# Staging a down pass eight steps ahead, and splitting the mixers' last contraction into an early and a late term

## The chip, the cores and the metric

The kernel runs on one core of a Trainium2 chip. The metric is the device time of one execution in microseconds (us); the figure for a kernel is the median of its runs. The core has five engines that each work through their own queue in order: TensorE (PE, matrix products; its weight loads are listed as PEld), VectorE (DVE), ScalarE (ACT), GpSimd (POOL) and SyncE (SP, which here only issues transfers). Transfers are issued from the queues of SP, ACT and POOL, and run on the core's 16 DMA engines.

## The reference

A decoder trunk of two residual layers over x of 1 x 1024 x 1024 float32. Layer A (even) is a causal differential attention beside a pooling mixer; layer C (odd) is a sliding-window attention with 16 query heads, a learned sink per head and an output projection. Each ends with a gated MLP that has a causal convolution of width 3:

```python
def swa_layer(x, norm_g, w_in, q_g, k_g, sinks, w_out):
    ...
    o = sliding_window_attention(q, k, v, sinks).astype(x.dtype)
    return x + o @ w_out

def conv_glu_ffn(x, norm_g, w_up, conv_w, conv_b, w_down):
    S = x.shape[1]
    h = rms_norm(x, norm_g) @ w_up
    hp = jnp.pad(h, ((0, 0), (CONV_W - 1, 0), (0, 0)))
    c = conv_b
    for j in range(CONV_W):
        c = c + conv_w[j] * hp[:, j:j + S]
    gate, up = jnp.split(c, 2, axis=-1)
    return x + (jax.nn.silu(gate) * up) @ w_down
```

with D_MODEL 1024 and D_FF 2816. So w_up is 1024 x 5632 and w_down 2816 x 1024.

## The kernel before

**Products.** Every float32 operand is split into a high part (an ACT copy, L130) and a low part (a DVE subtraction, L131, some on POOL), and a product is three matmuls: high by high, high by low, low by high. The MLP's products go by the seven products of Strassen's scheme on quarters, so sums and differences of quarters are formed before they are split.

**Stages**, by the time of the profiled execution: layer A 0 to 417, its up pass to 864 and down pass to about 1100; layer C to 1453, its up pass to about 1880 and down pass to the end.

**Order.** Instructions are written by the program in one order, and a scheduler moves them, engine by engine, by a simulated time and by the priorities that the code gives (`urgent(offset)`: the larger, the earlier). A tile comes from a ring of fixed size by its tag (x 8 tiles, xg 16, r 3, wr 2, ws 8, b 11, and PSUM banks s 3, q 3, d 2): who asks for a tile waits until the one that had it is done.

**The down pass** (`ffn_down`) forms the products p in the order 1, 5, 6, 3, 7, 2, 4, each over K = 11 steps k; a step is 12 matmuls of 128x512. `fetch` (L538, L545) puts the weights of a step into a staging tile by an SP transfer, from tags that `stages` lists: for product 1 the first two pairs of steps in wr, the later ones in r. The gated input comes from DRAM (gd) on POOL's queue into the tiles b, xg and hf (L551 to L570), and so does the residual x (L566). `prepare` forms the sum or difference that a product needs (`combine`, L573) and splits both operands (L130, L131). `lead`, after each step, fetches 9 steps ahead (FETCH) and prepares 3 ahead (AHEAD). The products' results are added to x on DVE (L632). In product 5 the weights' sums go into tiles that are kept (`held`, `sums`), since products 6 and 3 use them again.

**The mixers' ends.** `contract` (matmuls at L122, addition into x at L271) multiplies the attention's output by a part of the output projection, block by block (d of 8, half h of 2 of the positions), and adds each block to x. A generator yields beside the attention's main work (`weave`), so its matmuls fill the time in which TensorE would wait. In layer C the 16 heads are four groups of operands; groups 0 and 1, and then group 2 alone, are contracted beside the attention of the last group; the last group's contraction is `last`, one half at a time, with the norm of the next stage (`after`: L294 to L308) fed block by block.

Of the kernel before, what the change touches and what calls it, by code (L numbers as in the profile page):

```python
# [20 lines left out]
P = 128  # L21
# [36 lines left out]
AHEAD = 3  # L58
FETCH = 9

# [7 lines left out]
class Trunk:  # L68
# [190 lines left out]
    def contract(self, ws, gs, x, after=None, banks="dq", halves=(0, 1)):  # L259
# [4 lines left out]
        for n, (d, h) in enumerate(order):  # L264
# [7 lines left out]
                if after is not None:  # L272
                    after(d, h, xs)
                    if d == ND - 1:
                        after(None, h, None)

    def scaled_begin(self, idx, spill):
# [236 lines left out]
    def ffn_down(self, layer, xs, gd, after, begin=lambda part: None):  # L514
# [7 lines left out]
        pairs = {1: (0, lo), 6: (0, lo), 3: (K, lo), 2: (K, lo), 4: (K, hi)}  # L522
        raws, ops = {}, {}
        stages = {p: ("r", "wr", "r", "wr", "r") for p in (5, 6, 3, 7, 2)}
        stages[1], stages[4] = ("wr", "wr", "r", "r", "r"), ("r",)
        taken = dict.fromkeys(stages, 0)
# [30 lines left out]
        sums = [held[k // 2][:, (k % 2) * HALF:(k % 2 + 1) * HALF] for k in range(K)]  # L557
        x = [self.big("x") for _ in range(ND)]
        for k in range(EARLY, K):
            nc.gpsimd.dma_start(b11[k], g(k, hi))  # L560
        for k in range(K):
            if k < EARLY:
                nc.gpsimd.dma_start(b11[k], g(k, hi))
            nc.gpsimd.dma_start(b12[k], g(k, lo))  # L564
        for d in range(ND):
            nc.gpsimd.dma_start(x[d][:], xs[d * P:(d + 1) * P, :])  # L566
        for k in range(K):
            nc.gpsimd.dma_start(b22[k], g(K + k, lo))
        for k in range(K):
            nc.gpsimd.dma_start(b21[k], g(K + k, hi))  # L570

        def combine(out, a, b, op=ALU.subtract):
# [7 lines left out]

        def prepare(p, k):
            r = raws.pop((p, k))
            with self.urgent(9000):
# [8 lines left out]
                elif p == 3:  # L592
                    l, m = combine(sums[k], r, sums[k]), b22[k]
                elif p == 7:
                    l = combine(r[0], r[0], r[1])
                    m = combine(b22[k], b22[k], b12[k])
                elif p == 2:
                    l, m = r, b21[k]
                else:
                    l, m = r, combine(b21[k], b21[k], b11[k])  # L600
                ops[p, k] = operand(l), operand(m)

# [10 lines left out]
        def product(p):  # L613
# [15 lines left out]
            for m in range(4):  # L629
                xm = x[d0 + m][:, cols]  # L630
                with self.urgent(12000):
                    nc.vector.tensor_tensor(out=xm, in0=banks[p][m][:], in1=xm, op=ALU.add)  # L632
# [5 lines left out]
        def lead(n):  # L638
            if n + FETCH < len(seq):
                fetch(*seq[n + FETCH])  # L640
            if n + AHEAD < len(seq):
                prepare(*seq[n + AHEAD])

        for n in range(FETCH):
            fetch(*seq[n])
        for n in range(AHEAD):
            prepare(*seq[n])
# [343 lines left out]
    def layer_a(self, w, norm, bd, after):  # L991
# [80 lines left out]
        def last(h, after):  # L1072
            if h == 0:
                ws.extend(self.load_split(I["a_out"][2 + i]) for i in range(2))
            return self.contract(ws, [self.halves(am[i]) for i in (2, 3)], x, after, "qs" if h else "q", (h,))

# [95 lines left out]
    def layer_c(self, w0, norm, rest, xd, after):  # L1172
# [22 lines left out]

        x, sp = [], []

        def project_out():
# [3 lines left out]
            for gs in ((0, 1), (2,)):  # L1202
                ws = [self.load_split(I["c_out"][2 * g + t]) for g in gs for t in range(2)]
                yield from self.contract(ws, [m for g in gs for m in sp[g]], x, banks="d")

# [190 lines left out]
```

## Time and profile before

| what | value |
|---|---|
| runs | 2132.19, 2134.98, 2140.15 us; median 2134.98 |
| the profiled execution's own time | 2133.47 us |
| its span, first to last instruction | 2131.5 us |
| mean granted clock of TensorE | 0.982 |
| busy: PE / PEld / DVE / ACT / POOL | 2017.4 / 1718.2 / 1611.6 / 1107.7 / 257.9 us |
| moved by DMA | 216.97 MB, mean 102 GB/s |

A row of single instructions gives start and duration in us, engine, line, operation, the tile written and the tiles read, shapes and how many, and in brackets how long the engine was idle before it and what ended that. A row of a stretch gives its bounds and length, the busy time of each engine with the number of instructions, the clock granted to TensorE, the busy share of the 16 DMA engines and GB/s. A row of waits gives engine, tile and line, what it waited for, the sum, how many times, and the longest. A line's number can be that of a helper, such as L130, L131 or L271, that many places call.

### The profile page before, as it was taken

What the parts mean: (1) busy time and instruction counts of PE and PEld (TensorE: products, weight loads), DVE (VectorE), ACT (ScalarE), POOL (GpSimd) and SP (SyncE); (2) the same over time, 40 slices, a digit from 0 to 9 for tenths busy, and PEclk for the clock granted to TensorE, in tenths of its full rate; (3) what the DMA queues carried; (4) which work ended last, traced back from release to release, by engine and by line L of the source; (5) the groups of instructions that cost most, each with busy time, mean ns of one, the idle gap of its engine ahead of it and who ended that gap; (6) DMA issues with size and microseconds to landing.
All of it is one profiled execution on the core that took longest, in us unless ns stands there. A gap on an engine that the chain in (4) does not pass through costs nothing.

```text
span 2131.5 us, 28465 instructions
## 1 busy us (share of the span) xinstructions
PE 2017.4 (95%) x10440; PEld 1718.2 (81%) x10440; DVE 1611.6 (76%) x2890; ACT 1107.7 (52%) x2115; POOL 257.9 (12%) x449
## 2 busy tenths in 40 slices
PE   8999999889999999789999989898999999979999
PEld 6999877677888888678789987776788888867787
DVE  6677787877778777698863887787877777759875
ACT  5476755454445554335445876644645555444343
POOL 0322442000000002300013330200000000021000
PEclk9999999999999999999999999999999999999999
DMA  4210221302222224762421110211222222268242
GB/s 168 90 50 22 69 95 56 119 30 89 89 83 76 80 89 163 296 219 92 146 100 41 51 39 32 89 60 60 89 77 82 79 89 89 87 222 328 89 163 85
DMA packets 82333, 216.97 MB, mean 102 GB/s; under 512 B 9360, under 2 KB 9872, under 8 KB 82192
## 3 DMA queue, kind: packets, MB, share of 16 engines
q1 hardware_dynamic: 65296, 169.00, 22.9%
q0 software_dynamic: 9984, 33.56, 4.3%
q10 hardware_dynamic: 6912, 12.59, 1.6%
q8 instruction: 82, 1.34, 0.3%
q14 instruction: 59, 0.48, 0.1%
HBM read 173.17 MB, written 41.94 MB: 101 GB/s over the span
## 4 chain that ended last, share of the span: by engine, by line
PE 83%; DVE 8%; ACT 4%; issue 2%; DMA 2%; POOL 1%; SPq 0%; ACTq 0%; DVEq 0%; POOLq 0%
PE pss L339 22%; PE psq L339 12%; PE pss L610 8%; PE psq L610 6%; PE psd L679 6%; PE psd L122 6%; PE psd L610 5%; PE psd L339 4%; PE pss L679 3%; PE psq L122 3%; PE psq L852 1%; PE pss L904 1%; PE pss L750 1%; PE pss L751 1%; DMA r<-in_dram 1%
## 5 line engine op out<-in xcount | busy, mean ns | idle before, releaser
L339 PE MATMUL pss<-xg,ws 128*128 128x512 f32 x1248 | 298.6, 392 | 16.9 <-DVE xg L131 9.2
L339 PEld LDWEIGHTS pss<-xg,ws 128*128 128x128 f32 x1248 | 235.5, 189 | 69.4 <-DVE xg L131 10.0
L610 PE MATMUL pss<-ws,ws 128*128 128x512 f32 x726 | 204.3, 398 | 34.1 <-ACT ws L130 25.3
L339 PE MATMUL pss<-T,ws 128*128 128x512 f32 x912 | 224.5, 389 | 3.4 <-ACT ws L130 3.4
L339 PEld LDWEIGHTS pss<-T,ws 128*128 128x128 f32 x912 | 171.1, 188 | 39.6 <-ACT ws L130 4.3
L610 PEld LDWEIGHTS pss<-ws,ws 128*128 128x128 f32 x726 | 138.4, 192 | 66.1 <-ACT ws L130 26.9
L679 PE MATMUL psd<-ws,xg 128*128 128x256 f32 x1344 | 184.0, 285 | 2.2 <-DVE hms L688 1.7
L610 PE MATMUL psq<-ws,ws 128*128 128x512 f32 x660 | 185.3, 392 | 0.0
L679 PEld LDWEIGHTS psd<-ws,xg 128*128 128x128 f32 x1344 | 171.4, 191 | 4.7 <-DVE hms L688 2.3
L339 PE MATMUL psq<-xg,ws 128*128 128x512 f32 x696 | 169.5, 392 | 0.0
L131 DVE TENSOR_TENSOR ws<-hf,ws 128x512 fp32r<-128x512 f32 x160 | 109.6, 689 | 73.3 <-ACT ws L130 73.1
L122 PE MATMUL psd<-xg,ws 128*128 128x512 f32 x576 | 152.4, 402 | 3.7 <-DVE x L271 2.8
L339 PEld LDWEIGHTS psq<-xg,ws 128*128 128x128 f32 x696 | 131.9, 190 | 27.6
L130 ACT ACTIVATE ws<-wr 128x512 fp32r<-128x512 f32 (+1 forms) x158 | 115.5, 735 | 72.3 <-PE pss L339 33.4
L610 PEld LDWEIGHTS psq<-ws,ws 128*128 128x128 f32 x660 | 125.3, 190 | 26.4
L610 PE MATMUL psd<-ws,ws 128*128 128x512 f32 x462 | 140.2, 397 | 0.8 <-DVE ms L241 0.8
L130 ACT ACTIVATE ws<-hf 128x512 fp32r<-128x512 f32 x160 | 99.9, 629 | 76.1 <-PE psq L339 33.3
L564 POOL DMA_DIRECT2D xg<-gd x22 | 12.1, 550 | 995.8 <-PE pss L339 994.2
L131 POOL TENSOR_TENSOR ws<-wr,ws 128x1024 fp32r<-128x1024 f32 x38 | 95.0, 2508 | 287.7 <-ACT ws L130 247.0
L347 DVE SCALAR_TENSOR_TENSOR x<-x,conv,x 128x1023 f32<-128x1023 f32 x80 | 102.6, 1282 | 30.0 <-ACT x L346 29.8
L122 PEld LDWEIGHTS psd<-xg,ws 128*128 128x128 f32 x576 | 104.8, 190 | 25.2 <-DVE x L271 5.1
L130 ACT ACTIVATE ws<-xg 128x512 fp32r<-128x512 f32 x104 | 63.0, 624 | 109.1 <-PE psd L610 74.1
(258 smaller groups left out, 4105.6 us busy)
## 6 DMA issues: line engine op xcount, KB each, us to landing
wr<-in_dram SPq DMA_DIRECT2D x102, 512.0 KB, 3.6
gd<-x SPq DMA_DIRECT2D x40, 512.0 KB, 2.6
x<-in_dram SPq DMA_DIRECT2D x38, 512.0 KB, 4.4
r<-in_dram SPq DMA_DIRECT2D x34, 512.0 KB, 3.7
r<-in_dram SPq DMA_DIRECT2D x64, 256.0 KB, 3.6
xd<-x ACTq DMA_DIRECT2D x48, 256.0 KB, 2.0
xg<-gd POOLq DMA_DIRECT2D x44, 256.0 KB, 5.4
b<-gd POOLq DMA_DIRECT2D x44, 256.0 KB, 9.0
```

What stands on the lines that cost most here:

```text
L122: self.nc.tensor.matmul(out, a, b, start=(k == 0), stop=(k == n - 1))
L130: nc.scalar.activation(hi, raw, AF.Copy)
L131: (eng or nc.vector).tensor_tensor(out=lo, in0=raw, in1=hi.bitcast(F32), op=ALU.subtract)
L339: nc.tensor.matmul(bank[:], a, b, start=start and k == 0, stop=k == n - 1, skip_group_check=open)
L347: nc.vector.scalar_tensor_tensor(out=c[:, 1:], in0=hr[:, :S - 1], scalar=cw(1), in1=c[:, 1:], op0=ALU.mult, op1=ALU.add)
L564: nc.gpsimd.dma_start(b12[k], g(k, lo))
L610: nc.tensor.matmul(banks[p][m][:], l, r, start=opens and n == 0, stop=closes and n == 2, skip_group_check=p != 2)
L679: self.nc.tensor.matmul(out, a, m[:, d % 4, :], start=(n == 0), stop=(n == 23))
L750: nc.tensor.matmul(out, q[:, qs], his[m][:, ks], start=True, stop=False)
L751: nc.tensor.matmul(out, q[rows, qs], lo[rows, ks], start=False, stop=True)
L852: nc.tensor.matmul(po[:, :256], tt[:, kb * P:(kb + 1) * P], v, start=(b == 0 and t == 0), stop=(b == j and t == 1))
L904: nc.tensor.matmul(pu[:], a, b, start=d + n == 0, stop=d == ND - 1 and n == 2)
```

## The change

In `ffn_down` the weights of product 1's later steps are staged in x tiles; `fetch` runs 14 steps ahead; `prepare` is cut in two: `gather` forms the sums and differences 8 steps ahead (LEAD), `prepare` splits them, 3 ahead as before, at a higher priority; the POOL loads are written behind the first fetches, and x is taken after those x tiles.

In layers A and C the second half of the last contraction goes through the new `contract_late`: for each block, the term whose operands are older opens the bank (six banks at the start, alternately q and s), and the newer term closes it. In layer C the third group contracts only its first half beside the attention; the second half becomes the early term, and eight additions into x disappear, since both terms accumulate in one bank.

```diff
-FETCH = 9
+LEAD = 8
+FETCH = 14
...
+    def contract_late(self, early, late, x, after, h, banks="qsqsqs"):
+        nc, n = self.nc, len(banks)
+        po = {}
+        def part(d, terms, first):
+            if first:
+                po[d] = self.bank(banks[d % n])
...
+                for a, b in ((ah, bh), (ah, bl), (al, bh)):
+                    k += 1
+                    nc.tensor.matmul(po[d][:], a, b, start=first and k == 1, stop=not first and k == total)
+        for d in range(n):
+            yield 0.65 * len(early[0])
+            part(d, early, True)
+        for d in range(ND):
+            yield 0.65 * (len(late[0]) + len(early[0]))
+            part(d, late, False)
+            xs = x[d][:, h * HALF:(h + 1) * HALF]
+            with self.urgent():
+                nc.vector.tensor_tensor(out=xs, in0=po[d][:], in1=xs, op=ALU.add)
+            after(d, h, xs)
+            if d + n < ND:
+                part(d + n, early, True)
+        after(None, h, None)
...
-        stages[1], stages[4] = ("wr", "wr", "r", "r", "r"), ("r",)
+        stages[1], stages[4] = ("wr", "wr", "x", "x", "x", "x"), ("r",)
...
-        def prepare(p, k):
+        def gather(p, k):
             r = raws.pop((p, k))
             with self.urgent(9000):
...
+            parts[p, k] = l, m
+
+        def prepare(p, k):
+            l, m = parts.pop((p, k))
+            with self.urgent(12000):
                 ops[p, k] = operand(l), operand(m)
...
-                with self.urgent(12000):
+                with self.urgent(15000):
                     nc.vector.tensor_tensor(out=xm, in0=banks[p][m][:], in1=xm, op=ALU.add)
...
+            if n + LEAD < len(seq):
+                gather(*seq[n + LEAD])
...
         def last(h, after):
             if h == 0:
                 ws.extend(self.load_split(I["c_out"][6 + t]) for t in range(2))
-            return self.contract(ws, g3, x, after, "qs" if h else "q", (h,))
+                return self.contract(ws, g3, x, after, "q", (h,))
+            return self.contract_late((held, sp[2]), (ws, g3), x, after, h)
```

The lines move: splits L130/L131 become L131/L132, `combine` L573 becomes L592, `fetch` L538/L545 become L571/L578, the matmuls of `contract` L122 become L123, those of `contract_late` are L294, the transposes of layer C L1148 become L1191, the up pass's matmuls L339 become L372 and those of the down pass L610 become L634.

**SP's queue at the start of the first down pass.** in_dram is w_down; wr_8381 and wr_8423 are weights of product 5 (steps 1 and 3), r_8282, r_8284 and r_8286 those of product 1 from step 4 on (two steps each), gd the store of the gated input. Before:

```order
L545 DMA wr_8381<-in_dram 128x512 x2
L360 DMA gd_72<-x_8054 128x1024
L545 DMA wr_8423<-in_dram 128x512 x2
L538 DMA r_8282<-in_dram 128x2x512
L538 DMA r_8284<-in_dram 128x2x512
L538 DMA r_8286<-in_dram 128x2x512
L318 DMA conv_14348<-in_dram 128x176
```

With the change, where wr_8396 is product 5's step 6, r_8230, r_8236 and r_8354 its steps 0, 2 and 4, and x_8222 to x_8228 product 1's steps 4 to 10:

```order
L578 DMA wr_8396<-in_dram 128x512 x2
L578 DMA r_8230<-in_dram 128x512
L571 DMA x_8222<-in_dram 128x2x512
L571 DMA x_8224<-in_dram 128x2x512
L571 DMA x_8226<-in_dram 128x2x512
L571 DMA x_8228<-in_dram 128x512
L578 DMA r_8230<-in_dram 128x512
L578 DMA r_8236<-in_dram 128x512 x2
L578 DMA r_8354<-in_dram 128x512 x2
```

The last wr load ahead of product 1's later weights stays ahead of them, half of r_8230 joins it, and all of product 1's weights now go in one row, with product 5's behind them.

**DVE a little later, in product 1.** ws are split operands, xg_8212 to xg_8214 the kept sums of product 5, b the gated input. Before:

```order
L131 TENSOR_TENSOR ws_8384<-r_8284,ws_8384 128x512
L573 TENSOR_TENSOR b_8195<-xg_8206,b_8195 128x512
L131 TENSOR_TENSOR ws_8387<-b_8196,ws_8387 128x512
L131 TENSOR_TENSOR ws_8405<-r_8284,ws_8405 128x512
L131 TENSOR_TENSOR ws_8408<-b_8197,ws_8408 128x512
L573 TENSOR_TENSOR b_8196<-xg_8207,b_8196 128x512
L573 TENSOR_TENSOR b_8197<-xg_8208,b_8197 128x512
L131 TENSOR_TENSOR ws_8426<-r_8286,ws_8426 128x512
```

With the change:

```order
L132 TENSOR_TENSOR ws_8401<-x_8224,ws_8401 128x512
L592 TENSOR_TENSOR xg_8212<-r_8230 128x512
L592 TENSOR_TENSOR xg_8213<-wr_8333 128x512
L592 TENSOR_TENSOR b_8195<-xg_8206,b_8195 128x512
L132 TENSOR_TENSOR ws_8404<-b_8196,ws_8404 128x512
L132 TENSOR_TENSOR ws_8424<-x_8224,ws_8424 128x512
L592 TENSOR_TENSOR xg_8213<-r_8236 128x512
L592 TENSOR_TENSOR b_8196<-xg_8207,b_8196 128x512
L132 TENSOR_TENSOR ws_8427<-b_8197,ws_8427 128x512
L132 TENSOR_TENSOR ws_8447<-x_8226,ws_8447 128x512
L592 TENSOR_TENSOR xg_8214<-r_8354 128x512
```

Sums of product 5 (from r_8230, r_8236 and r_8354) now stand between the splits of product 1's steps 6, 7 and 8.

**TensorE in the tail of layer C, at the last transposes.** hf and g are split attention weights and values, L1148 (L1191) the transposes, psq and pss banks. Before:

```order
L122 MATMUL psq_14001<-g_13761,ws_13853 128x512
L122 MATMUL psq_14001<-g_13760,ws_13854 128x512
L1148 MATMUL psq_14097<-idn,t_14069 128x128 x4
L1148 MATMUL psq_14102<-idn,t_14069 128x128 x4
L122 MATMUL psq_14107<-hf_14108,g_10368 128x256
```

With the change (six rows for each of the two pss banks, all of one kind, and the last bank of the contraction's first half):

```order
L123 MATMUL psq_13925<-g_13696,ws_13790 128x512
L294 MATMUL pss_14150<-xg_13338,ws_13388 128x512
...
L294 MATMUL pss_14164<-xg_13338,ws_13395 128x512
L123 MATMUL psq_13937<-g_13696,ws_13783 128x512
...
L1191 MATMUL psq_14033<-idn,t_14005 128x128 x4
L1191 MATMUL psq_14038<-idn,t_14005 128x128 x4
L123 MATMUL psq_14043<-hf_14044,g_10368 128x256
```

Twelve matmuls of the early term now stand ahead of the transposes. Six more (pss_14136) stand earlier, and in the rest of the tail 18 stand before the split of the last group is used, and 12 behind it.

More of the change, by code (lines that the diff above doesn't have):

```diff
@@ L275, in contract @@
                         after(None, h, None)
+    def contract_late(self, early, late, x, after, h, banks="qsqsqs"):
[4 more added lines that the diff above has]
+                po[d] = self.bank(banks[d % n])
+            ws, gs = terms
+            total = 3 * len(ws)
+            k = 0
+            for (wh, wl), g in zip(ws, gs):
+                ah, al = wh[:, d * P:(d + 1) * P], wl[:, d * P:(d + 1) * P]
+                bh, bl = g(h)
+                for a, b in ((ah, bh), (ah, bl), (al, bh)):
[14 more added lines that the diff above has]
+        after(None, h, None)
     def scaled_begin(self, idx, spill):
@@ L522, in ffn_down @@
         pairs = {1: (0, lo), 6: (0, lo), 3: (K, lo), 2: (K, lo), 4: (K, hi)}
-        raws, ops = {}, {}
+        raws, parts, ops = {}, {}, {}
         stages = {p: ("r", "wr", "r", "wr", "r") for p in (5, 6, 3, 7, 2)}
-        stages[1], stages[4] = ("wr", "wr", "r", "r", "r"), ("r",)
+        stages[1], stages[4] = ("wr", "wr", "x", "x", "x", "x"), ("r",)
         taken = dict.fromkeys(stages, 0)
@@ L557, in ffn_down @@
         sums = [held[k // 2][:, (k % 2) * HALF:(k % 2 + 1) * HALF] for k in range(K)]
[L558 to L570, printed above, removed]
         def combine(out, a, b, op=ALU.subtract):
@@ L645, in ffn_down @@
             fetch(*seq[n])
+        for k in range(EARLY, K):
+            nc.gpsimd.dma_start(b11[k], g(k, hi))
+        for k in range(K):
+            if k < EARLY:
+                nc.gpsimd.dma_start(b11[k], g(k, hi))
+            nc.gpsimd.dma_start(b12[k], g(k, lo))
+        x = [self.big("x") for _ in range(ND)]
+        for d in range(ND):
+            nc.gpsimd.dma_start(x[d][:], xs[d * P:(d + 1) * P, :])
+        for k in range(K):
+            nc.gpsimd.dma_start(b22[k], g(K + k, lo))
+        for k in range(K):
+            nc.gpsimd.dma_start(b21[k], g(K + k, hi))
+        for n in range(LEAD):
+            gather(*seq[n])
         for n in range(AHEAD):
@@ L1074, in last @@
                 ws.extend(self.load_split(I["a_out"][2 + i]) for i in range(2))
-            return self.contract(ws, [self.halves(am[i]) for i in (2, 3)], x, after, "qs" if h else "q", (h,))
+                return self.contract(ws, [self.halves(am[i]) for i in (2, 3)], x, after, "q", (h,))
+            two = [([ws[i]], [self.halves(am[2 + i])]) for i in range(2)]
+            return self.contract_late(*two, x, after, h)
         ws = []
@@ L1194, in split_o @@
             return [(lambda h, t=t: (hs[h][0][:, t, :], hs[h][1][:, t, :])) for t in range(2)]
-        x, sp = [], []
+        x, sp, held = [], [], []
         def project_out():
@@ L1203, in project_out @@
                 ws = [self.load_split(I["c_out"][2 * g + t]) for g in gs for t in range(2)]
-                yield from self.contract(ws, [m for g in gs for m in sp[g]], x, banks="d")
+                if gs == (2,):
+                    held.extend(ws)
+                    yield from self.contract(ws, sp[2], x, lambda *a: None, "d", (0,))
+                else:
+                    yield from self.contract(ws, [m for g in gs for m in sp[g]], x, banks="d")
         side = dense()
```

## The prediction

> **What bounds the kernel now.** I read the page first (busy times, then the chain that ended last), then the list of what TensorE waits for, then busy time by stretch around each place that the edits touch, and last single instructions there. From the page:
>
> ```profile
> span 2131.5 us, 28465 instructions
> PE 2017.4 (95%) x10440; PEld 1718.2 (81%) x10440; DVE 1611.6 (76%) x2890; ACT 1107.7 (52%) x2115; POOL 257.9 (12%) x449
> PE 83%; DVE 8%; ACT 4%; issue 2%; DMA 2%; POOL 1%; SPq 0%; ACTq 0%; DVEq 0%; POOLq 0%
> ```
>
> PE is busy 2017.4 of 2131.5 us and is 83% of the chain. No edit removes a matmul, so all there is to win is PE's 114 us without work and the slow clock that follows its gaps. From the list of waits of the whole run, the two rows on the down pass:
>
> ```profile
> PE pss L610 <- ACT ws L130: 25.3, 4, 12.0
> PE pss L610 <- DVE ws L131: 8.8, 3, 4.1
> ```
>
> 34 us in two down passes. Where they lie, by stretch (length, then busy time of PE, PEld, DVE, ACT, POOL, granted clock, DMA share, GB/s); the first five rows are the first pass, the last two the second:
>
> ```profile
> 870.00:883.00 13.00, 1.44 (x5) 0.88 (x4) 7.09 (x8) 4.18 (x6) 6.35 (x12) 0.71 1.01 370
> 883.00:904.00 21.00, 21.00 (x87) 16.63 (x86) 17.55 (x30) 9.66 (x18) 7.74 (x15) 0.94 1.03 399
> 904.00:935.00 31.00, 29.73 (x132) 24.30 (x131) 29.97 (x50) 10.19 (x19) 0.83 (x2) 1.00 0.78 272
> 935.00:941.00 6.00, 1.85 (x6) 1.24 (x7) 6.00 (x11) 2.96 (x6) 0.00 (x0) 0.66 0.57 186
> 941.00:1100.00 159.00, 156.45 (x700) 129.29 (x699) 125.18 (x205) 76.47 (x136) 5.45 (x4) 0.98 0.35 118
> ...
> 1905.00:1920.00 15.00, 2.96 (x12) 2.11 (x11) 7.97 (x8) 4.99 (x7) 7.56 (x15) 0.66 0.98 350
> ...
> 1942.00:1975.00 33.00, 29.42 (x129) 23.71 (x127) 31.18 (x52) 12.24 (x22) 1.50 (x3) 0.99 0.73 259
> ```
>
> Each pass has two holes. The first (870 to 883) has all 16 DMA engines full: TensorE waits for weights. The second (935 to 941) has DVE at 6.00 of 6: TensorE waits for sums and splits. DVE is full for the 31 us before it too. After 941 PE is at 156.45 of 159: nothing is left there.
>
> **The down pass: the first hole.** Its instructions:
>
> ```profile
> 867.51 0.69 DVE L573 TENSOR_TENSOR xg<-wr 128x512 f32<-128x512 f32 x1 [6.39 <-PE pss L339]
> ...
> 868.24 0.81 SPq L545 DMA_DIRECT2D wr<-in_dram  x2
> 869.09 3.35 SPq L538 DMA_DIRECT2D r<-in_dram  x3
> ...
> 880.06 0.63 ACT L130 ACTIVATE ws<-r 128x512 fp32r<-128x512 f32 x1 [7.48 <-DMA r<-in_dram]
> 883.79 0.63 ACT L130 ACTIVATE ws<-r 128x512 fp32r<-128x512 f32 x1 [0.59 <-DMA r<-in_dram]
> 887.54 0.63 ACT L130 ACTIVATE ws<-r 128x512 fp32r<-128x512 f32 x1 [1.56 <-DMA r<-in_dram]
> ...
> 882.21 1.22 PE L610 MATMUL pss<-ws,ws 128*128 128x512 f32 x2 [11.56 <-ACT ws L130]
> 1918.90 1.22 PE L610 MATMUL pss<-ws,ws 128*128 128x512 f32 x2 [12.04 <-ACT ws L130]
> ```
>
> The combine at 867.51 reads a wr tile; only then may SP's next wr load go (868.24), and the loads of product 1's later weights, which TensorE needs, stand behind it on the same queue (869.09). They land 3.7 us apart per 512 KB (880.06, 883.79, 887.54), about 141 GB/s, because POOL's loads of b and x run beside them; by queue for 870 to 900, POOL's is q0:
>
> ```profile
> q0 software_dynamic: 2271, 7.82, 68.1%
> q1 hardware_dynamic: 1986, 3.80, 34.1%
> ```
>
> The change gives these weights an x tile instead of an r tile, but r was not what they waited for. In the changed order the wr load that waits for the same combine still stands ahead of them, and one more 256 KB load of product 5 with it. 256 KB at 141 GB/s is 1.9 us: the first hole grows from 11.6 to 13.5 us, in both passes. POOL's loads keep their order until long after, so they leave no more bandwidth.
>
> **The down pass: between the holes.** With sums eight steps ahead, three sums of product 5 stand on DVE, an in-order queue, ahead of splits that product 1 needs: one ahead of step 6's, one ahead of step 7's, one ahead of step 8's. What they read lands behind all of product 1's weights: from 881.9 (880.04 and 1.9) there are 512, 512, 256, 256, 512 and 512 KB to the last, 2.5 MB at 141 GB/s, so 18.6 us: 900.6. Before, DVE had only this wait there:
>
> ```profile
> 895.38 0.69 DVE L573 TENSOR_TENSOR xg<-r 128x512 f32<-128x512 f32 x1 [3.46 <-DMA r<-in_dram]
> 895.99 0.68 DVE L573 TENSOR_TENSOR xg<-wr 128x512 f32<-128x512 f32 x1
> ...
> 939.49 0.69 DVE L131 TENSOR_TENSOR ws<-b,ws 128x512 fp32r<-128x512 f32 x1
> ...
> 903.67 0.69 PE pss L610 x3
> ...
> 940.24 2.08 PE pss L610 x4
> ...
> 944.87 0.91 PE pss L610 x4
> ```
>
> From 895.38 to 939.49, the split that lets product 6 begin at 940.24, DVE does 71 operations, 0.62 us each. In the changed order 64 operations lie between the sum that waits for 900.6 and the same split: 64 × 0.62 = 39.7, so 940.3. By TensorE: step 8 of product 1 waits for about 902.5, steps 8 to 10 are 36 matmuls (12 take 2.73 us, row 864.76 below), so product 5 begins near 910 where it began at 903.67, and its 11 steps of 2.73 end at 940. Both ways product 6 begins where it did.
>
> So the second hole's 5.4 us move forward into product 1 (about 5 us) and the first hole (1.9); the sum is +0.1. What goes is the slow clock after the long gap at 936: product 6's first step took 4.63 us (940.24 to 944.87) instead of 2.73, −1.9. The three new gaps are shorter, 1 to 3 us; the row 1422 below shows half clock after two gaps of 1.19 and 1.71 us, so I charge +1.3 for them. Per pass −0.5, two passes **−1**. The bounds: if no sum is late, product 5 begins at 905.6 (903.67 and 1.9) and product 6, if DVE allows, 30.0 later, 4.6 sooner than before, with the clock's 1.9: −6.5. If the weights land as computed and the second hole stays too, +7.
>
> The Trainium skill, page "TensorE: Matmul & The Clock Gate", section "What's actually happening", has the clock halved only after an idle window of about 3.4 us. This trace shows the half clock after gaps of 1.19 and 1.71 us close together. By the page the new gaps would cost no clock, and the two passes would give −3.6 instead of −1.
>
> **Layer A's contraction.** The order of TensorE's instructions there is the same before and after: six banks already stood open with their older term, since the scheduler had moved it forward. Zero, and nothing to lose.
>
> **Layer C's contraction.** Side blocks of the third output group, 48 matmuls of the second half, leave the stretch before 1417 and go into the tail. The rows (chain of waits, then TensorE's and DVE's instructions, then stretches):
>
> ```profile
> 864.76 2.73 PE pss L339 x12
> ...
> 1397.90 2.75 PE psd L122 x12
> ...
> 1404.11 2.72 PE psd L122 x12
> ```
>
> ```profile
> L271 DVE TENSOR_TENSOR x<-psd,x x8: 678/684/692, 1400.3 to 1416.7; 128x512 f32<-128x512 f32 x8
> ```
>
> ```profile
> 1398.00:1420.00 22.00, 20.67 (x105) 17.29 (x103) 18.80 (x49) 12.41 (x34) 0.00 (x0) 1.00 0.17 56
> 1422.00:1424.00 2.00, 2.00 (x9) 1.81 (x9) 1.97 (x10) 1.04 (x4) 0.00 (x0) 0.50 0.70 246
> ```
>
> ```profile
> 1418.77 0.38 PE L122 MATMUL psq<-hf,g 128*128 128x256 f32 x1 [1.19 <-ACT hf L130]
> 1421.57 1.65 PE L122 MATMUL psq<-hf,g 128*128 128x256 f32 x6 [1.71 <-DVE hf L131]
> 1432.64 0.39 PE L122 MATMUL psq<-hf,g 128*128 128x256 f32 x1 [1.61 <-ACT hf L130]
> 1437.92 0.85 PE L122 MATMUL psq<-hf,g 128*128 128x256 f32 x5 [0.34 <-DVE hf L131]
> 1440.72 0.50 PE L122 MATMUL psq<-g,ws 128*128 128x512 f32 x1 [0.98 <-ACT g L130]
> 1452.78 1.40 PE L339 MATMUL pss<-xg,ws 128*128 128x512 f32 x5 [0.89 <-DVE x L271]
> ```
>
> What leaves: to 1410 TensorE sets the pace, and 24 of the 48 matmuls are on the chain (1397.90 and 1404.11): 5.5 us. From there DVE does, and four of its eight psd additions (0.6 us each by the spacing at 895.38) go: 2.4. Together 7.9; the attention's own DVE work (18.80 of 22 us) will not let all of it through, so I take 6.5.
>
> What comes: of the 48, six go into the 1.71 us wait (free); 12 (2.7 us) stand ahead of the last transposes, whose result is awaited at 1432.64; I count half of that 1.61 us as slack, so +1.8. Six (1.4 us) enter where 0.34 us was idle: +0.9, with some slack behind them. Twelve (2.7) fill the wait for the split g, 1.95 us from the last attention product to 1440.72: +0.8. The last 12 stand behind 1440.72 beside the 48 of the late term, which fill 10.9 of the 12.1 us to 1452.78; the rest is the last block's addition, which still follows: +2.7. Sum +6.2. The slow clock at 1422 may go with its gap (half of 1.5): −0.7. C gives −6.5 + 6.2 − 0.7 = **−1**; the bounds are −9 (all leaves, the waits hide all that comes) and +6 (nothing leaves but the work).
>
> **Sum.** −1 − 1 = −2 against the profiled execution, 2133.47 us (span 2131.5 and 2 around it): 2131.5. It stands 1.5 below the median of the runs, 2134.98, so I write 2132.
>
> **Rivals.** *The holes close.* The sums for product 6 are there in time and product 1's three waits do not come, because loads land sooner than at 141 GB/s; the first hole stays as it is. Then per pass the second hole (5.4 and 1.9 of clock) goes, and C keeps −1: 2133.5 − 14.6 − 1 = 2118. For it: DVE had 3.46 us free at 895. Against: DMA at 1.03 with POOL taking two thirds to 904, and DVE full to 941.
>
> *The early sums block.* In-order DVE waits for product 5's staged weights as computed, and the second hole stays because sums for product 6 now stand ahead of its first splits. Per pass +1.9 + 5 + 0: with the tail of C at +1, 2148. It decides if the last of the three loads lands after about 900 and more than 70 DVE operations remain. For it: the landings. Against: the order shows 64 operations, and adds and splits ahead of sums.
>
> *C alone gains.* The waits of C take up nearly all that comes, −7, and the passes give −1: 2125.5. For it: 6.7 us of idle in six rows. Against: the last 12 matmuls have no idle to go into.
>
> **How the numbers follow.** No change 0.52, the holes close 0.19, the early sums block 0.17, C alone 0.12. A measurement here tells 0.5% (10.7 us) from no change: faster is below 2124.3, slower above 2145.6. Faster: 0.19 and a third of C alone, 0.23. Slower: 0.17 and 0.02 of the forecast's upper end, 0.19. Same: 0.58. The likeliest case alone spans 2124 to 2141; to leave out no more than 2 in 10 the range reaches half into both outer rivals: 2119 to 2146.
>
> **What would show it.** Right: a wait of 13 to 14 us before step 4 of product 1 in both passes; then waits of 1 to 3 us in product 1 on DVE's splits; product 6 beginning without a wait near 940 and at full clock; in C, TensorE done with the late term some 2 to 3 us later than DVE's spare additions save. Wrong: the first wait at or below 11.6 us, no wait in product 1 after its step 4, a wait of 4 us still before product 6, or the stage from 1393 to 1453 more than 4 us shorter or longer.

## The result and the profile after

The changed kernel takes 2121.6 us (median of its runs) where the kernel before, timed beside it, takes 2133.59: a ratio of 0.9939, 95% interval 0.9923 to 0.9956. So it is faster, by 12 us. Executions far above the others of their kernel (here one of five, at 2288.93 us, and later the profiled one of e16, at 6568.74) are left out. The profiled execution took 2124.41 us, the longest of those counted; before it was 2133.47. From the page of the changed kernel:

```profile
span 2122.2 us, 28436 instructions
PE 2016.3 (95%) x10440; PEld 1719.0 (81%) x10440; DVE 1602.0 (75%) x2882; ACT 1107.2 (52%) x2115; POOL 257.8 (12%) x449
```

TensorE does the same 10440 matmuls in 1.1 us less, and the span is 9.3 us shorter: most of the gain is in TensorE's gaps. The place of a gain is found fastest by the start of the first matmul of each stage. The rows of this table are differences of such starts, in us (the last row ends with the start of the last matmul):

| stretch | before | after | difference |
|---|---|---|---|
| start to layer A's up pass | 417.60 | 417.01 | −0.6 |
| layer A's up pass | 433.85 | 433.76 | −0.1 |
| its down pass, products 1, 5, 6 | 119.55 | 119.74 | +0.2 |
| its down pass, the rest | 131.00 | 130.95 | 0.0 |
| layer C, to its up pass | 350.77 | 350.48 | −0.3 |
| layer C's up pass | 434.89 | 426.69 | **−8.2** |
| its down pass, products 1, 5, 6 | 119.95 | 119.66 | −0.3 |
| its down pass, the rest | 119.45 | 119.45 | 0.0 |

No edit is in an up pass, and yet 8.2 of the 9.3 us are in one. The places that were edited (the mixers of A and C, and the two down passes) give 1.0 us together.

**The down pass.** TensorE's waits in the changed kernel (sum, times, longest):

```profile
PE pss L634 <- ACT ws L131: 27.0, 2, 13.5
PE pss L634 <- DVE ws L132: 7.3, 5, 2.9
```

The two rows add up to 34.3 us; the corresponding rows of before had 25.3 and 8.8, so 34.1. The waits were moved, not removed. Single instructions of the first pass (TensorE; then the sums of product 5 on DVE):

```profile
883.46 1.22 PE L634 MATMUL pss<-ws,ws 128*128 128x512 f32 x2 [13.49 <-ACT ws L131]
895.11 1.95 PE L634 MATMUL pss<-ws,ws 128*128 128x512 f32 x4 [2.69 <-DVE ws L132]
903.00 1.20 PE L634 MATMUL pss<-ws,ws 128*128 128x512 f32 x4 [0.54 <-DVE ws L132]
892.55 0.69 DVE L592 TENSOR_TENSOR xg<-r 128x512 f32<-128x512 f32 x1 [5.40 <-DMA r<-in_dram]
900.45 0.69 DVE L592 TENSOR_TENSOR xg<-r 128x512 f32<-128x512 f32 x1 [1.51 <-DMA r<-in_dram]
```

The first wait has grown from 11.56 to 13.49 us, and product 1 has new waits while DVE stands before sums whose weights have not landed. By stretch, in the columns of the prediction's rows:

```profile
870.00:883.00 13.00, 0.00 (x0) 0.00 (x0) 5.16 (x7) 2.93 (x4) 6.24 (x12) 0.68 1.01 372
883.00:904.00 21.00, 17.30 (x56) 13.30 (x57) 13.30 (x21) 7.73 (x14) 5.36 (x10) 0.79 1.03 396
904.00:935.00 31.00, 31.00 (x137) 25.36 (x136) 31.00 (x53) 12.06 (x21) 2.65 (x5) 1.00 0.69 251
935.00:941.00 6.00, 6.00 (x28) 4.99 (x27) 5.82 (x10) 3.03 (x6) 0.00 (x0) 1.00 0.37 131
```

The second hole is gone: TensorE is busy all of 935 to 941, at full clock. But 883 to 904, where it was busy all 21 us, has 3.7 us without work and a clock of 0.79. Product 6 begins at 940.58; before, its second hole ended at 940.24.

**Layer C's up pass.** Before, TensorE ran into the second half's norm here:

```profile
1469.00 0.60 PE L239 MATMUL psd<-idn,hf 128*128 128x128 f32 x4
1478.33 0.50 PE L339 MATMUL pss<-xg,ws 128*128 128x512 f32 x1 [2.13 <-ACT xg L130]
1484.11 1.65 PE L339 MATMUL pss<-xg,ws 128*128 128x512 f32 x3 [4.59 <-DVE xg L131]
```

The row of 1469.00 is the transposes of that norm; the two waits behind it, 2.13 and 4.59 us, are for the scaled and split x of the second half. After:

```profile
1437.97 2.50 PE L294 MATMUL psq<-g,ws 128*128 128x512 f32 x5 [2.55 <-DVE g L132]
1451.94 8.55 PE L372 MATMUL pss<-xg,ws 128*128 128x512 f32 x37
1460.33 0.60 PE L240 MATMUL psd<-idn,hf 128*128 128x128 f32 x4
1477.72 0.98 PE L372 MATMUL pss<-xg,ws 128*128 128x512 f32 x3 [1.54 <-DVE xg L132]
```

The transposes stand 37 matmuls into the up pass instead of 71 (1460.33 less 1451.94 is 8.4 us; before, 1469.00 less 1452.78 was 16.2), and one wait of 1.54 us is left of 6.72. The same 40 us from the up pass's first matmul, before and then after:

```profile
1453.00:1493.00 40.00, 33.28 (x139) 26.89 (x139) 29.51 (x57) 13.29 (x22) 0.00 (x0) 0.87 0.09 33
```

```profile
1452.00:1492.00 40.00, 38.46 (x176) 31.62 (x175) 29.36 (x57) 15.10 (x25) 0.00 (x0) 1.00 0.19 66
```

176 matmuls against 139. The 139 took 33.28 us at a clock of 0.87; at the later kernel's 38.46/176 they would take 30.4. So 2.9 us of slow clock and 5.2 us of waits are gone: 8.1 of the 8.2.

**Why the norm comes sooner.** Rows of ACT and DVE at the end of layer C, before:

```profile
1439.61 1.06 ACT L130 ACTIVATE g<-t 128x1024 fp32r<-128x1024 f32 x1
1440.69 0.60 ACT L254 ACTIVATE rbc<-psd 128x512 f32<-128x512 f32 x1
1441.84 5.38 DVE L308 SCALAR_TENSOR_TENSOR x<-x,par,rbc 128x512 f32<-128x512 f32 x8
```

and after:

```profile
1430.76 0.60 ACT L255 ACTIVATE rbc<-psd 128x512 f32<-128x512 f32 x1 [2.47 <-PE psd L251]
1432.15 1.06 ACT L131 ACTIVATE g<-t 128x1024 fp32r<-128x1024 f32 x1
1431.39 5.39 DVE L341 SCALAR_TENSOR_TENSOR x<-x,par,rbc 128x512 f32<-128x512 f32 x8 [2.24 <-ACT rbc L255]
1436.69 1.22 DVE L132 TENSOR_TENSOR g<-t,g 128x1024 fp32r<-128x1024 f32 x1
```

rbc is the first half's norm factor, spread over the partitions; g is the last attention group's second half, being split; the eight scalings apply rbc to the first half of x. Before, ACT did g first and rbc behind it, so DVE's 5.4 us of scalings fell behind the split of g and right ahead of the eight additions (L271) that the second half's norm waits for. These began from 1447.14 to 1456.74, with the splits of the scaled x between them. Now rbc comes first, ten us earlier, and the scalings stand ahead of the split of g; the additions (L304) begin from 1442.64 to 1452.70. I call these two orders *late* (before) and *early* (after). The scheduler chose the order; no line of the change asks for it.

### The profile page after: what moved, and what is told of

Same layout as the page of the kernel before. It is cut to its first block, busy times and chain, and to the rows that moved or that the text cites. A ratio compares the mean times of both kernels' runs of the same rounds, so it can differ in the third digit from the quotient of the medians.

```text
span 2122.2 us, 28436 instructions
## 1 busy us (share of the span) xinstructions
PE 2016.3 (95%) x10440; PEld 1719.0 (81%) x10440; DVE 1602.0 (75%) x2882; ACT 1107.2 (52%) x2115; POOL 257.8 (12%) x449
## 4 chain that ended last, share of the span: by engine, by line
PE 82%; DVE 7%; ACT 4%; DMA 3%; issue 2%; POOL 1%; SPq 0%; ACTq 0%; DVEq 0%; POOLq 0%
PE pss L372 22%; PE psq L372 12%; PE pss L634 7%; PE psq L634 6%; PE psd L720 6%; PE psd L123 5%; PE psd L372 5%; PE psd L634 4%; PE pss L720 3%; PE psq L123 2%; PE psq L893 1%; DMA b<-gd 1%; PE pss L945 1%; PE pss L791 1%; PE pss L792 1%
## 5 line engine op out<-in xcount | busy, mean ns | idle before, releaser
L372 PE MATMUL pss<-xg,ws 128*128 128x512 f32 x1248 | 297.0, 391 | 10.8 <-DVE xg L132 6.1
L372 PEld LDWEIGHTS pss<-xg,ws 128*128 128x128 f32 x1248 | 234.5, 189 | 62.3 <-DVE xg L132 7.0
L634 PE MATMUL pss<-ws,ws 128*128 128x512 f32 x726 | 209.5, 398 | 34.3 <-ACT ws L131 27.0
L372 PE MATMUL pss<-T,ws 128*128 128x512 f32 x912 | 224.6, 390 | 3.4 <-ACT ws L131 3.4
L372 PEld LDWEIGHTS pss<-T,ws 128*128 128x128 f32 x912 | 171.1, 188 | 39.6 <-ACT ws L131 4.2
L634 PEld LDWEIGHTS pss<-ws,ws 128*128 128x128 f32 x726 | 138.0, 192 | 66.1 <-ACT ws L131 27.9
L634 PE MATMUL psq<-ws,ws 128*128 128x512 f32 x660 | 191.5, 393 | 0.0
L372 PE MATMUL psq<-xg,ws 128*128 128x512 f32 x696 | 168.5, 391 | 0.0
L132 DVE TENSOR_TENSOR ws<-hf,ws 128x512 fp32r<-128x512 f32 x160 | 109.6, 689 | 73.4 <-ACT ws L131 73.1
L372 PEld LDWEIGHTS psq<-xg,ws 128*128 128x128 f32 x696 | 131.1, 188 | 27.2
L131 ACT ACTIVATE ws<-wr 128x512 fp32r<-128x512 f32 (+1 forms) x156 | 114.2, 737 | 68.9 <-PE pss L372 23.7
L634 PEld LDWEIGHTS psq<-ws,ws 128*128 128x128 f32 x660 | 125.4, 190 | 26.4
L634 PE MATMUL psd<-ws,ws 128*128 128x512 f32 x462 | 145.6, 397 | 0.8 <-DVE ms L242 0.8
L123 PE MATMUL psd<-xg,ws 128*128 128x512 f32 x528 | 140.2, 404 | 3.1 <-DVE x L272 2.3
L131 ACT ACTIVATE ws<-hf 128x512 fp32r<-128x512 f32 x160 | 100.0, 630 | 76.1 <-PE psq L372 33.3
L132 POOL TENSOR_TENSOR ws<-wr,ws 128x1024 fp32r<-128x1024 f32 x38 | 95.0, 2506 | 284.8 <-ACT ws L131 242.3
L123 PEld LDWEIGHTS psd<-xg,ws 128*128 128x128 f32 x528 | 97.1, 192 | 23.2 <-DVE x L272 4.3
L372 PE MATMUL psq<-T,ws 128*128 128x512 f32 x456 | 115.6, 390 | 0.0
```

The costliest lines, as they stand in the source:

```text
L123: self.nc.tensor.matmul(out, a, b, start=(k == 0), stop=(k == n - 1))
L131: nc.scalar.activation(hi, raw, AF.Copy)
L132: (eng or nc.vector).tensor_tensor(out=lo, in0=raw, in1=hi.bitcast(F32), op=ALU.subtract)
L372: nc.tensor.matmul(bank[:], a, b, start=start and k == 0, stop=k == n - 1, skip_group_check=open)
L634: nc.tensor.matmul(banks[p][m][:], l, r, start=opens and n == 0, stop=closes and n == 2, skip_group_check=p != 2)
```

## The experiments

All kernels were timed against the kernel before on the same chip. C is the stretch from layer C's start to its up pass, and *tail* the part of it from the matmul that uses the last transposes (1432.64 before) on. P0 and P1 are products 1, 5 and 6 of the two down passes. All stretches are from one profiled execution.

| kernel | median us | ratio, 95% | C | its tail | up pass C | P0 | P1 | order in C |
|---|---|---|---|---|---|---|---|---|
| before | 2133.59 | | 350.8 | 20.1 | 434.9 | 119.6 | 120.0 | late |
| after | 2121.6 | 0.9939, 0.9923–0.9956 | 350.5 | 28.2 | 426.7 | 119.7 | 119.7 | early |
| after_again | 2123.39 | 0.9944, 0.9926–0.9961 | 349.3 | 28.1 | 426.7 | 119.6 | 120.0 | early |
| e1_staging_only | 2133.25 | 0.9997, 0.9987–1.0007 | 347.9 | 20.1 | 434.5 | 119.8 | 119.8 | late |
| e2_deferral_only | 2132.42 | 0.9994, 0.9984–1.0003 | 349.7 | 23.6 | 435.6 | 121.7 | 119.8 | late |
| e5_adds_kept | 2133.89 | 0.9996, 0.9987–1.0005 | 351.3 | 21.6 | 434.5 | 121.6 | 119.5 | late |
| e4_left_out | 2127.64 | 0.9967, 0.9954–0.9979 | 346.5 | 20.1 | 433.6 | 120.1 | 119.5 | late |
| e17_order_only | 2134.29 | 0.9994, 0.9982–1.0006 | 360.4 | 26.8 | 426.0 | 119.7 | 120.1 | early |
| e16_deferral_order | 2128.71 | 0.9964, 0.9952–0.9975 | | | | | | early |
| e16b_deferral_order | 2129.63 | 0.9974, 0.9961–0.9987 | 356.2 | 31.2 | 426.0 | 119.8 | 119.9 | early |
| e22_order_in_a | 2131.58 | 0.9978, 0.9967–0.9989 | 355.5 | 26.6 | 426.6 | 120.6 | 119.2 | early |
| e24_sums_on_pool | 2123.94 | 0.9936, 0.9918–0.9954 | 356.2 | 30.1 | 426.0 | 114.8 | 113.8 | early |
| e12_sums_on_pool_r | 2121.05 | 0.9937, 0.9919–0.9955 | 346.7 | 28.1 | 426.6 | 120.5 | 122.4 | early |
| e23_sums_on_pool_c | 2114.66 | 0.9909, 0.9893–0.9925 | 350.6 | 29.9 | 428.0 | 114.6 | 115.0 | early |

(e16b is the kernel of e16 again, on another chip, for its stretches.) C ahead of its tail differs between executions even where ACT and DVE do the same in the same order: by 3.0 us between before and e17, and by up to 3.8 us among after, after_again and e12. Differences of C of that size are not read below; the tail, the up pass and the medians are.

### Each half alone

The staging without the mixers' edits, and the mixers' edits without the staging:

```diff
# e1: the changed kernel, with the mixers as before, for instance
-            return self.contract_late((held, sp[2]), (ws, g3), x, after, h)
+            return self.contract(ws, g3, x, after, "qs" if h else "q", (h,))
# e2: the kernel before, with contract_late and its calls in layers A and C
```

> The change without its mixer part: the down pass as changed, both layers' contractions as before. Theory A (the gain comes from layer C's third group alone, whose second half leaves the attention; staging gives nothing): within 2 us of the kernel before, first wait of each down pass 13.5 us, product 5 about 7 us later than before and product 6 where it was. Theory B (the staging gives part of it, above all in the second pass): 4 us or more below the kernel before.

> The kernel before with the mixer part alone: down pass as before, first wait 11.6 us, and 4 to 5 us before product 6. Theory A: 9 us below the kernel before, all of it between layer C's last contraction and the end of the second norm's first use (the up pass of layer C from 434.9 to about 427 us). Theory B: 5 us or less.

Measured: neither gains (0.9997 and 0.9994, both intervals across 1), yet together they give 0.9939. If gains were additive, the two would give −0.1%. In e1 the down pass shows the changed kernel's waits, and the up pass those of before (waits of 850 to 1100, then of 1449 to 1500):

```profile
PE pss L634 <- ACT ws L131: 13.5, 1, 13.5
...
PE pss L372 <- DVE xg L132: 4.2, 1, 4.2
PE pss L372 <- ACT xg L131: 2.1, 1, 2.1
```

In e2, ACT has the late order, though the deferred matmuls fill the tail there too:

```profile
1433.86 1.06 ACT L130 ACTIVATE g<-t 128x1024 fp32r<-128x1024 f32 x1
1435.34 0.60 ACT L254 ACTIVATE rbc<-psd 128x512 f32<-128x512 f32 x1 [0.42 <-PE psd L250]
```

Each of the two theories fails on one run: A on e2, which was to gain 9 us, and B on e1, which was to gain 4 or more. So the gain belongs to neither edit; what both together have is the early order. That leaves two questions: does the order make the gain, and what does the deferral do for it?

### Is the deferral's gain in the additions or the matmuls?

e5 keeps the deferral in layer C but adds into x twice per block, as before; e4 leaves the 48 deferred matmuls out altogether. In both, layer A is left as before.

```diff
# e5, against e2
-            return self.contract_late((held, sp[2]), (ws, g3), x, after, h)
+            def both():
+                yield from self.contract(held, sp[2], x, lambda *a: None, "s", (1,))
+                yield from self.contract(ws, g3, x, after, "qs", (1,))
+            return both()
# e4, against e2: the third group's second half isn't contracted at all
+            return self.contract(ws, g3, x, after, "qs", (h,))
```

> As the deferral alone, but the third group's second half goes through banks of its own in the tail and is added to x by eight additions on VectorE, as before. Theory A (what counts is that the matmuls leave the stretch before the first half's last block, so that the first norm and then the second come earlier): 6 to 9 us below the kernel before; the wait in the up pass of layer C stays under 3 us. Theory C (what counts is that eight additions, 4.8 us of VectorE, are gone): at most 3 us below the kernel before, and the wait back near 6.7 us.

> As the deferral alone, but the third group's second half of layer C is not computed at all (48 matmuls, 10.9 us of TensorE, are left out). If the moved matmuls lie fully in TensorE's waits: the time of the deferral alone. If they lie on the path: 11 us below it. Theory A, from the tail of the changed kernel (TensorE 12.00 of 12 us busy at the end, waits of 2.6 us left): about half, 5 us below it.

Measured: e5 is no faster than before (0.9996), with C 1.7 us longer than in e2, which is less than two executions of the same order can differ by. e4's 48 matmuls are 10.9 us of TensorE at 2.73 us per 12; leaving them out brings the tail 3.5 us and the up pass 2.0 us below e2, and the medians 4.8 us. So about half of them lie on the path, as expected. Both kernels have the late order, and in both the up pass is within 1.3 us of before, so neither the additions nor the matmuls are where the 8.2 us went.

### The order alone, with and without the deferral

A one-column copy on ACT that reads rbc and writes to the place where the split of g goes makes ACT do rbc first. It adds 0.2 us of work and changes nothing that is computed, since the split overwrites it.

```diff
+        def rest():
+            self.nc.scalar.activation(pairs[1][0][:, 0, 0:1], self.nrbc[:, 0:1], AF.Copy)
+            cut(1)
...
-        self.finish(x, main, side, last, after, RATES_C[3], lambda: cut(1))
+        self.finish(x, main, side, last, after, RATES_C[3], rest)
# e17: on the kernel before.  e16, e16b: on e2
```

> The kernel before with the forced order alone, neither edit of the change. Theory D: the up pass of layer C shorter by 7 to 8 us; the tail of layer C up to 2 us longer, since the last split comes later; 5 to 8 us below the kernel before. Theory F (the order helps only with the deferral, which puts matmuls into the wait for the split): 3 us or less.

> The deferral alone (down pass as before) with one forced order: a one-column copy on ScalarE makes the split of the last group's second half wait for the broadcast of the first half's norm. Theory D (the gain is that order: the norm's broadcast ahead of the split, so that the eight scalings and then the second half's norm come earlier; the two edits only happened to bring it about together): 8 us below the kernel before, the up pass of layer C near 427 us and its wait near 1.5 us. Theory E (the gain needs the staged down pass itself): as the deferral alone, within 3 us of the kernel before.

> The deferral with the forced order once more, for its profile (the first one's profiled execution was disturbed): wait in the up pass of layer C near 1.5 us, that up pass near 427 us, layer C's own length within 2 us of the changed kernel's; down passes as in the kernel before.

> The changed kernel once more, beside the two others: 11 to 13 us below the kernel before, and the same times of its stages within 1 us.

Measured: the order shortens the up pass by 8.9 us in both (426.0), so the up pass is explained: it hangs on the order alone. What the order costs stands in layer C. In e17 that grows by 9.6 us and nothing is won (0.9994), as the theory had it by which the order helps only with the deferral. 3.0 of the 9.6 lie ahead of the tail, where every engine has the order of before, and are chance; the tail is longer by 6.6. TensorE there (the last group's contraction):

```profile
1445.09 0.50 PE L122 MATMUL psq<-g,ws 128*128 128x512 f32 x1 [2.01 <-ACT g L130]
1450.33 2.50 PE L122 MATMUL psq<-g,ws 128*128 128x512 f32 x5 [3.16 <-DVE g L131]
```

It waits for g, which now stands behind the scalings, and has nothing else to do. With the deferral it has: the 48 matmuls do not need g. e16 and e16b gain 0.36% and 0.26% without any staging; e16's interval is clear of those of e17 and e2, e16b's overlaps them slightly. They do not reach the changed kernel, timed again beside e16b: C is 6.9 us longer than there, against 2 expected. 3.1 us of it are in the tail, because the forced order is a stricter one than the scheduler's own. From e16b, ACT and TensorE:

```profile
1434.73 0.60 ACT L254 ACTIVATE rbc<-psd 128x512 f32<-128x512 f32 x1 [1.51 <-PE psd L250]
1435.60 1.06 ACT L130 ACTIVATE g<-t 128x1024 fp32r<-128x1024 f32 x1
1441.94 2.50 PE L293 MATMUL psq<-g,ws 128*128 128x512 f32 x5 [3.57 <-DVE g L131]
```

Counted from the tail's start, rbc comes 1.9 us later than in the changed kernel, where TensorE does the broadcast that it reads (L251) ahead of five attention matmuls and six of the early term; g waits for it, and TensorE for g, 3.57 us instead of 2.55. The other 3.8 us lie ahead of the tail. There ACT and DVE of the two kernels go through the attention in different orders, from some 195 us into the layer on; whether that or chance makes the 3.8 us is not shown.

So this much is shown: the early order takes 8 to 9 us out of the up pass, and lengthens C's tail by 6.6 us where nothing is deferred. With the deferral the kernel gains by the order, by the medians. Part of that is the wait that the deferred matmuls fill: TensorE waits 2.55 us for g in the changed kernel, 2.01 and 3.16 in e17. The larger part is ahead of the tail: there e2, e16b and the changed kernel are 4.6, 5.7 and 8.3 us shorter than before, and the changed kernel's 8.3 are what its tail, 8.0 longer, costs. As e1, which defers nothing, is 2.9 us shorter there, how much of this the deferral gives is known only roughly. What is not shown at all is why the scheduler finds the early order only with the staging. It works in the program's order with simulated times, and the down passes that the staging edits lie before and after layer C; e12 below, another edit in the down pass on top of e2, tips it as well. I found no rule in it.

### The same order in layer A

Layer A's end is built alike and has the late order in all these kernels: its up pass is 434 us, C's early one 427. e22 forces it there (and, as in e16, in C), on the changed kernel.

```diff
-        mixes = [self.big("x") for _ in range(AH - 1)] + [self.big("rbc")]
+        mixes = [self.big("x") for _ in range(AH - 1)] + [self.big("xg")]
...
+        def rest():
+            self.nc.scalar.activation(am[3][0][:, HALF:HALF + 1], self.nrbc[:, 0:1], AF.Copy)
+            self.split_half(mixes[3], am[3], 1)
```

> The changed kernel with the same order forced in layer C (where it already is) and in layer A, where the last head's result moves from the tile that the norm's broadcast needs into an xg tile. Theory D: layer A's up pass loses its 2.1 and 4.6 us waits as layer C's did: 6 to 8 us below the changed kernel, about 2114. Against it: layer A's tail is longer by the later split, and less than 3 us are left.

Measured: A's up pass does shorten, 433.8 to 428.0 us, but it starts at 425.19 instead of 417.01, so the two together lose 2.4; with C's forced order, 355.5 instead of 350.5, the kernel is slower than the changed one (0.9978), where 6 to 8 us of gain on it were expected. The row that says why:

```profile
414.38 1.12 PE L926 MATMUL psd<-idn,xg 128*128 128x128 f32 x4 [11.38 <-DVE xg L918]
```

In A the scalings and the first half's splits stand ahead of DVE's own work on the last head, and TensorE waits 11.38 us for that. That nothing is left in A which could be deferred to cover it is argued, not tried.

### What bounds the first hole: sums on GpSimd

The staging in x tiles moved the down pass by 0.2 us. To see what it is worth once DVE's in-order queue is out of its way, product 5's sums of weights go to GpSimd: in e24 on e22, in e23 on the changed kernel with the order in C forced, and in e12 on e2, so with product 1's weights in r tiles as before.

```diff
-                    l = combine(sums[k], r[0], r[1], ALU.add)
+                    l = sums[k]
+                    nc.gpsimd.tensor_tensor(out=l, in0=r[0], in1=r[1], op=ALU.add)
```

> The kernel of the run with the order in layer A, with product 5's eleven sums of weights on GpSimd instead of VectorE. If product 1's waits come from sums that stand ahead of its splits on VectorE (as predicted and seen), they go, and eleven operations (6.6 us) leave the full stretch of VectorE: product 6 begins 6 to 8 us earlier in each pass, 12 us or more below that run, about 2102. If GpSimd's sums hold up the loads that stand behind them on its queue, the first wait grows from 13.5 us and the gain is below 3 us.

> The changed kernel with product 5's sums of weights on GpSimd and the order of layer C forced (as the changed kernel has it by itself); layer A as changed. From the run with the order in layer A: the first wait falls from 13.5 to about 6.5 us and product 3 begins 5 to 6 us sooner after the pass's start, in both passes. If that adds to layer C's gain: 11 us below the changed kernel, near 2110. If the scheduler gives layer C another order, or GpSimd's sums are late for product 5: 2115 or more.

> The deferral with product 5's sums on GpSimd, but product 1's weights staged in r tiles as before the change. If the x tiles bring nothing (as the run of the staging alone shows) and the loads' place on SP's queue is what counts: within 2 us of the run with the x tiles, first wait 6.5 us or less. If with the sums out of VectorE's way the deeper staging comes to bear: 4 us or more above it.

Measured: in e24 and e23, P0 and P1 shorten by 4.7 to 5.9 us each (against e22 and the changed kernel), and e23 is the fastest kernel of the study: 2114.66 us, 0.9909, some 9 us below the changed kernel on the same chip. Both gain less than expected (e24 7.6 us on e22 instead of 12 or more, e23 9 instead of 11); the last section shows what may be part of the reason. e23's wait for product 1's weights in the first down pass:

```profile
PE pss L635 <- ACT ws L131: 6.4, 1, 6.4
```

The first wait is 6.4 us where it was 13.49. The reason stands on SP's queue; the changed kernel first, with the sum on DVE that its wr load waits for:

```profile
859.28 0.33 SPq L393 DMA_DIRECT2D gd<-x  x1
867.55 0.80 SPq L578 DMA_DIRECT2D wr<-in_dram  x2
868.87 3.14 SPq L571 DMA_DIRECT2D x<-in_dram  x4
...
866.83 0.69 DVE L592 TENSOR_TENSOR xg<-wr 128x512 f32<-128x512 f32 x1 [6.39 <-PE pss L372]
```

and e23, with its sum on GpSimd:

```profile
860.63 0.33 SPq L393 DMA_DIRECT2D gd<-x  x1
861.05 0.38 SPq L578 DMA_DIRECT2D r<-in_dram  x1
861.48 3.39 SPq L571 DMA_DIRECT2D x<-in_dram  x4
864.93 8.92 SPq L578 DMA_DIRECT2D r<-in_dram  x5
873.94 0.85 SPq L578 DMA_DIRECT2D wr<-in_dram  x2
...
869.07 1.30 POOL L607 TENSOR_TENSOR xg<-wr 128x512 f32<-128x512 f32 x1
```

In the changed kernel SP stands still from 859.6 to 867.55, since the sum that empties the wr tile begins at 866.83, itself held by the up pass; the x loads for product 1 stand behind it. With the sum on GpSimd, which is no sooner (869.07), the scheduler puts that wr load last, and the x loads start 7.4 us earlier. A stretch just there shows the DMA engines at work in time that was spare, the changed kernel and then e23:

```profile
860.00:865.00 5.00, 5.00 (x23) 4.15 (x23) 0.44 (x1) 0.00 (x0) 0.00 (x0) 1.00 0.28 111
```

```profile
860.00:865.00 5.00, 5.00 (x23) 4.14 (x23) 1.29 (x2) 0.60 (x1) 0.00 (x0) 1.00 0.91 282
```

e12 has the short first wait too, 6.4 us, but product 1's weights hold the r tiles. Product 5's loads into r begin at 879.61, where all but one of e23's begin at 864.93, and product 5 waits (SP; TensorE; then ACT, held by the sum on GpSimd):

```profile
879.61 9.55 SPq L577 DMA_DIRECT2D r<-in_dram  x6
...
904.57 0.79 PE L643 MATMUL pss<-ws,ws 128*128 128x512 f32 x1 [4.92 <-ACT ws L130]
903.37 0.63 ACT L130 ACTIVATE ws<-xg 128x512 fp32r<-128x512 f32 x1 [13.40 <-POOL xg L620]
```

Its P0 and P1 are 120.5 and 122.4 against e23's 114.6 and 115.0, and the kernel is 6.4 us slower than e23, where less than 2 was expected if the x tiles brought nothing. So the staging is worth 5.9 and 7.4 us in the two passes once the sums are off DVE, and nothing while they are on it (e1). And e12 is as fast as the changed kernel (0.9937) with no staging at all: it has the deferral and, unforced, the early order. From layer C's start to 40 us into its up pass, its ACT and DVE do the changed kernel's instructions in the same order, row for row, and tail and up pass take the same time (28.1 and 426.6). That is a second sign that the change's gain is the order.

## Why the prediction was right and wrong

The time is within the range, but the likeliest case, no change at 2132, missed: the kernel is faster by 0.6%. That the range held is luck: it reached down to 2119 for two rivals, and neither of them came.

- **The first hole** was to grow from 11.6 to 13.5 us in both passes: 13.49 and 13.5. The reason given, a wr load that waits for a sum and stands ahead of the weights on SP, is what e23 showed by moving it.
- **Between the holes.** The last of the late weights was to land at 900.6: DVE's sum began at 900.45, released by its transfer. Product 5 near 910: 910.41. Product 6 near 940 with no wait and at full clock: 940.58, clock 1.00. The waits in product 1 were to come to about 5 us. From the end of the first wait to product 5 it took 26.95 us (883.46 to 910.41) where it took 21.29 before; of these 5.7 us more, only 3.2 are waits (2.69 and 0.54), and the rest is mostly slow clock. Per pass −0.5 was forecast, +0.2 and −0.3 came. 0.9 of the difference rests on a misread row: 940.24 is not where product 6 began before, since four of its matmuls had run at 934.89, ahead of the long wait.
- The step named sums eight steps ahead as the cause of DVE's order. That reason was wrong: written with 3 steps of lead for the sums, 11 for the fetches and the old priorities, the changed code gives every engine the same order, row for row. Of the down pass's edits, only the x tiles and the deeper fetch that they need move instructions.
- **The charge for the clock** (+1.3 per pass) was for gaps of 1 to 3 us. The 2.69 us gap ended at 895.11, and this is the clock behind it:

```profile
895.00:897.00 2.00, 1.89 (x5) 1.51 (x6) 1.21 (x3) 0.00 (x0) 0.53 (x1) 0.57 1.03 400
897.00:899.00 2.00, 2.00 (x7) 1.57 (x6) 1.94 (x4) 0.20 (x1) 0.00 (x0) 0.58 1.04 398
```

Eight matmuls take 3.45 us (895.11 to 898.56) where full clock needs 1.82: +1.6. The Trainium skill, page "TensorE: Matmul & The Clock Gate", section "What's actually happening", has the clock fall only after an idle window of about 3.4 us. This trace disagrees: it fell after 2.69 us.

- **Layer A, zero:** right, −0.6 and −0.1, and kernels with the same order there start their up pass anywhere from 415.7 to 418.2.
- **Layer C** as far as its first matmul of the up pass: −1 forecast. With the late order kept (e2) it was −1.1. Cut at the matmul that uses the last transposes (1432.64 before), the forecast was −5.4 ahead of it and +4.4 behind; e2 has −4.6 and +3.5, the first of them no surer than the 3 us by which executions differ there. The changed kernel has −8.3 and +8.0, the scalings having moved into its tail, so that its −0.3 is near the forecast only as a sum.
- **The sum failed by a term that was not in it.** It counted layer C to 1453, the up pass's first matmul, and took the rest as unchanged. The second half's norm reaches 31 us further, to the wait that ended at 1484.11, and that is where the −8.2 us are. Every row needed for it stood in the trace of before: 2.13 and 4.59 us of waits and a clock of 0.87. What moved there stood in the changed order of ACT and DVE at the end of C, which was read for TensorE alone.

**The rivals.** *The holes close* (2118): fell, although the time came near it; the first hole grew, product 1 waited. *The early sums block* (2148): its waits came as computed, but the second hole went. *C alone gains* (2125.5): the nearest by place, and still not it, since the waits inside C did not hide what came.

**What would show it.** Three of the four signs came as written (first wait, waits in product 1, product 6). None of the listed signs looked at the up pass.

## What to carry to other kernels

Where a scheduler sets the order, compare the whole program's order on every engine, also at places that an edit does not touch: here the gain came from a swap of two ACT instructions that no line asked for, and each edit alone gave nothing. Carry a stage's sum through to the last wait that hangs on it, not to the next stage's first matmul. Here an order that brought one chain forward paid only where the engine that it holds up was relieved elsewhere (the 48 deferred matmuls; e17 and e22 without that gave nothing or lost), and earlier staging paid only where the transfers did not stand behind a load that waits for a busy engine.

## What the runs showed of the hardware that was not expected

GpSimd's addition of two 128x512 float32 tiles took 1.30 us (869.07 in e23), a little under twice DVE's 0.69. DVE's own work beside such additions became slower. From e23, the split of an x tile on DVE, and GpSimd's additions during it:

```profile
889.37 6.75 DVE L132 TENSOR_TENSOR ws<-x,ws 128x512 fp32r<-128x512 f32 x1 [0.83 <-ACT ws L131]
889.94 1.29 POOL L607 TENSOR_TENSOR xg<-wr 128x512 f32<-128x512 f32 x1
```

The split took 6.75 us where its neighbours take 0.68; GpSimd was at four more such additions between 888.68 and 895.56. In the two passes of e23, ten additions or subtractions of this size on DVE took 1.77 to 7.64 us; in the changed kernel none took more than 0.9. In the first pass TensorE's waits for DVE's splits came to 5.9 us instead of 3.8. So the sums were not simply off DVE's hands. That the pass became 5 us shorter all the same goes with the first wait, 6.4 us instead of 13.49.

That a single gap of 2.69 us, with the clock at 1.00 before it, is followed by 4 us at clocks of 0.57 and 0.58 was not expected either; the forecast had reasoned from two gaps close together.
